# Two-layer decoder step on one core: gathered rows of layer 0 freed later, number pairs from their own tile, rows held back at the norms

## The chip, the cores and the metric

The kernel runs on one core of a Trainium2 chip as one program. The metric is the device time of one execution in microseconds. The kernel before took 3266.15, 3272.88 and 3274.58 us in three runs, a median of 3272.88. A profiled execution of it took 3263.07 us, of which the span from the first to the last recorded instruction is 3261.4 us.

The core has these engines, each with a queue of its own that is worked off strictly in order: PE (TensorE, matrix products), DVE (VectorE), ACT (ScalarE), POOL (GpSimd, here almost only for issuing gathers) and SP (SyncE, which issues the plain DMAs). An instruction waits at the head of its queue for semaphores that other engines raise; whatever stands behind it waits too.

## The reference

One step of a decoder with two layers, over 512 prompt tokens and 8 sample tokens, 1024 wide, in float32:

```
layer 0:  x += gmlp(rmsnorm(x));             x += peer(rmsnorm(x))
layer 1:  x += diff_attention(rmsnorm(x));   x += peer(rmsnorm(x))

rmsnorm:  y = x * rsqrt(mean(x*x) + EPS) * g

peer:     q  = h @ w_q                       # 8 heads, two halves of 128
          s  = q . keys                      # 128 + 128 scores for each head
          the 16 best of each half, the 16 best sums of pairs -> 16 of 16384 experts
          g  = softmax(the 16 sums)
          act = gelu(u_tab[expert] . h)
          out = sum over 8*16 experts of  g * act * v_tab[expert]
```

So each token picks 8 x 16 experts of 16384 in each layer; an expert is one row of `u_tab` and one of `v_tab`, 1024 numbers each. Outputs are the new x, the new keys and values, and a state of the gMLP.

## The kernel before

**Tiles.** The 512 prompt tokens are four tiles x0 to x3 of 128 tokens, the samples a fifth. Each layer's front (gMLP or attention, then the query and the ranking of `peer_front`) runs in two groups: in layer 0 first tile 2, then tiles 0, 1, 3 and the samples; in layer 1 first tile 0, then 2, 3, 1.

**Two ways to the experts.** In each layer two tiles (0 and 1 in layer 0, 2 and 3 in layer 1) go the *dense* way, `dense_peer`: all 16384 experts are computed on PE, and the 128 chosen ones get their weight by a one-hot product, the gates. The other two tiles go the *gathered* way, `peer_tile`: for each of the 128 choices POOL gathers a row of `u_tab` for each of the 128 tokens (0.5 MB for a tile), DVE multiplies and sums it (L712), and later the same for a row of `v_tab`, which DVE adds to x (L719). That is 2 x 256 = 512 such DVE instructions of 1024 columns for a layer; the text calls each of them a *gathered row*. They go through five buffers (`gb`).

**The dense way** runs in four quarters of 32 blocks of 128 experts. `acts(q)` computes the activations W: for q = 0 plain products (L494), after that with operands split in two (L209 on ACT and L211 on DVE make the high and low half, L488, L489 and L491 are the products). `gates(q)` builds one-hot tables: for 32 tokens at a time DVE compares the chosen row numbers with 0, 1, ..., 31, two tokens side by side (L512), scales that by the two parts of the gate (L514), and PE multiplies it with a second one-hot table (`ohj`, L520 on DVE or L526 and L529 on ACT) into L533; DVE multiplies the result into W (L536). Then PE multiplies W with the rows of `v_tab` (L573), in the last quarter with both sides split in two (L569 to L571; L564 makes the low half of W, L211 that of `v_tab`, each through two pairs of buffers). `gates(q+1)` and `acts(q+1)` run between the products of quarter q.

**The ranking** of a tile is DVE work: searches for the 8 largest and their places in score tiles `s_uv` and the like (L366 to L395, `topk_rank`), then the pick (L408 to L451, `topk_pick`), which goes to ACT for one Exp. For a dense tile PE transposes the pick (`ps_sel`, L461), for the samples L692.

**What sets the order.** The gathered rows have no fixed place in DVE's queue. While the body is written down, `tick` appends instructions to a list of anchors, each k times, and `peer_tile` collects the rows (`pins`). At the end `pace` ties row n to the n-th anchor: it may not be placed ahead of it. That sets the order in which a scheduler, with a clock of its own, places instructions; no semaphore comes of it. More ticks on an instruction free more rows there. In layer 0 the anchors begin when the ranking of tile 2 is through and go on into the first group of layer 1, until `cur[0] = None`; all rows of layer 0 must be done before group 2 of layer 1 reads x2 and x3.

**The norms** end in `rstd`, a chain of 8 or 9 small DVE instructions for the reciprocal root (L128 to L140).

Of the kernel before, what the change touches and what calls it, by code (L numbers as in the profile page):

```python
# [11 lines left out]
HF = mybir.dt.float16  # L12
# [3 lines left out]
OP = mybir.AluOpType  # L16
# [19 lines left out]
def body(ctx: ExitStack, tc: tile.TileContext, a):  # L36
    nc = tc.nc
    V, SC, PE, GP, SY = nc.vector, nc.scalar, nc.tensor, nc.gpsimd, nc.sync
# [37 lines left out]
    stage, dd = [0], {}  # L76
# [27 lines left out]
    def tick(ins, k=1):  # L104
        if cur[0] is not None:
            anchors[cur[0]].extend([ins.ins.name] * k)

    def pace():
        for a_, p_ in zip(anchors, pins):
            for n, ins in enumerate(p_):  # L110
                tc.add_manual_dep(ins, a_[min(n, len(a_) - 1)], NOSYNC, reason="pace")


    def small(p, m, name, dt=F32, bufs=4):
# [8 lines left out]
    def rstd(ss, p, m, inv_n, out=None):  # L123
        ms = small(p, m, "rs_ms" + ("m" if m > 1 else ""), F32, 1 if m > 1 else 4)
        y = small(p, m, "rs_y" + ("m" if m > 1 else ""), F32, 1 if m > 1 else 6)
        t = small(p, m, "rs_t" + ("m" if m > 1 else ""), F32, 1 if m > 1 else 4)
        u = small(p, m, "rs_u" + ("m" if m > 1 else ""), F32, 1 if m > 1 else 4)
        V.tensor_scalar(ms, ss, inv_n * KAP, EPS * KAP, op0=OP.mult, op1=OP.add)  # L128
        V.tensor_scalar(y.bitcast(I32), ms.bitcast(I32), -0.5, C0, op0=OP.mult, op1=OP.add)
        for k in range(2):  # L130
            if m == 1:
                V.scalar_tensor_tensor(t, y, y, ms, op0=OP.mult, op1=OP.mult)
            else:
                V.tensor_tensor(t, y, y, op=OP.mult)
                V.tensor_tensor(t, t, ms, op=OP.mult)
            if k == 0:
                V.scalar_tensor_tensor(y, t, -C2, y, op0=OP.add, op1=OP.mult)
        V.scalar_tensor_tensor(u, t, -CA, t, op0=OP.add, op1=OP.mult)
        out = y if out is None else out
        V.scalar_tensor_tensor(out, u, CB, y, op0=OP.add, op1=OP.mult)  # L140
        return out

    def bcast_row(src, n, name, bufs=2, p=128):
# [63 lines left out]
    def split(w, k=1):  # L207
        wh = wp.tile([128, 8, 128], FR, name="wh", tag="wh", bufs=2)
        SC.activation(wh, w, AF.Copy)  # L209
        wl = wp.tile([128, 8, 128], FR, name="wl", tag="wl", bufs=2)  # L210
        tick(V.tensor_tensor(wl, w, wh.bitcast(F32), op=OP.subtract), k)  # L211
        return wh, wl

    def dense(w, nk, rhs, n, consume, f0=0, f1=None, steps=None):

        f1 = w.shape[0] if f1 is None else f1
        for f in range(f0, f1):
            ps = pm.tile([128, 512], F32, name="ps_d", tag="mm")
            for c0 in range(0, nk, 8):
                wt = wp.tile([128, 8, 128], F32, name="wt", tag="wt")  # L220
                SY.dma_start(wt, w[f, :, c0:c0 + 8, :])
                if isinstance(rhs, list):
                    wh, wl = split(wt, [1, 2, 1, 2][stage[0]])
                    for c in range(8):
                        PE.matmul(ps[:, :n], wh[:, c, :], rhs[0][:, c, :n], start=c == 0, stop=False)
                        PE.matmul(ps[:, :n], wh[:, c, :], rhs[1][:, c, :n], start=False, stop=False)
                    for c in range(8):
                        PE.matmul(ps[:, :n], wl[:, c, :], rhs[0][:, c, :n], start=False, stop=c == 7)
                else:
                    for c in range(8):  # L230
                        z = PE.matmul(ps[:, :n], wt[:, c, :], rhs[:, c0 + c, :n], start=c0 + c == 0,  # L231
                                      stop=c0 + c == nk - 1)
                    tick(z, [6, 6, 6, 3][stage[0]])
            consume(f - f0, ps)
            step([4, 6, 4, 5][stage[0]] if steps is None else steps)

# [232 lines left out]
    def dense_peer(layer, dpa, open_rest, open_odd, smp):  # L469
        hT = dd["hT"]  # L470
# [7 lines left out]
        def acts(q):  # L478

            W[q] = (odd if q % 2 else dpa).tile([128, QI, 256], F32, name="W", tag="W", bufs=1)  # L480
            for il in range(QI):
                u = wp.tile([128, 8, 128], F32, name="ub", tag="wt")
                SY.dma_start(u, a["peer_ut"][layer, q * QI + il].rearrange("p (c e) -> p c e", c=8))
                ps = pt.tile([128, 512], F32, name="ps_a", tag="tr")[:, :256]
                if q:
                    uh, ul = split(u, [2, 3][layer])
                    for c in range(8):
                        PE.matmul(ps, uh[:, c, :], hP[0][:, c, :], start=c == 0, stop=False)  # L488
                        PE.matmul(ps, uh[:, c, :], hP[1][:, c, :], start=False, stop=False)  # L489
                    for c in range(8):  # L490
                        PE.matmul(ps, ul[:, c, :], hP[0][:, c, :], start=False, stop=c == 7)  # L491
                else:
                    for c in range(8):
                        z = PE.matmul(ps, u[:, c, :], hT[:, c, :256], start=c == 0, stop=c == 7)  # L494
                    tick(z, [0, 1][layer])
                    if il == 1:
                        SC.activation(hP[0], hT[:, :, :256], AF.Copy)
                        V.tensor_tensor(hP[1], hT[:, :, :256], hP[0].bitcast(F32), op=OP.subtract)
                SC.activation(W[q][:, il, :], ps, AF.Gelu_apprx_tanh)  # L499
                yield  # L500

        def gates(q):

            selJ, selb = dd["sel"]
            sq = dpb.tile([128, 256], HF, name="selq", tag="selq", bufs=1)
            V.tensor_scalar(sq, selb[:, 0, :], float(-q * QI), None, op0=OP.add)
            for t0 in range(0, 256, 32):

                gi = dpb.tile([128, 2, 16, QI, 2], HF, name="gi", tag="gi", bufs=2)
                sv = [z[:, t0:t0 + 32].rearrange("p (m w) -> p m w", w=2)[:, :, None, :].to_broadcast([128, 16, QI, 2])  # L510
                      for z in (sq, selb[:, 2], selb[:, 3])]
                V.tensor_tensor(gi[:, 1], sv[0], iotaJ[:, None, :QI, :2].to_broadcast([128, 16, QI, 2]), op=OP.is_equal)  # L512
                for k in range(2):
                    V.tensor_tensor(gi[:, k], gi[:, 1], sv[1 + k], op=OP.mult)  # L514
                for t1 in range(t0, t0 + 32, 16):
                    ps = pt.tile([128, QI, 16], F32, name="ps_g", tag="tr")
                    for t2 in range(t1, t1 + 16, 8):
                        oh = dpb.tile([128, 128, 8], HF, name="ohj", tag="ohj", bufs=4)
                        if (t2 // 8) % 4 < ([2, 2][layer] if not q else 2 * J_DVE[layer][q]):
                            V.tensor_tensor(oh, selb[:, 1, None, t2:t2 + 8].to_broadcast([128, 128, 8]), iotaJ,  # L520
                                            op=OP.is_equal)
                        else:

                            oh = oh.rearrange("p j k -> p (j k)").rearrange("p (k j) -> p j k", k=8)
                            for k in range(8):
                                SC.activation(oh[:, :, k], iota128, AF.Abs, scale=-1.0,  # L526
                                              bias=selJ[:, t2 + k:t2 + k + 1])
                            oh2 = oh.rearrange("p j k -> p k j")
                            SC.activation(oh2, oh2, AF.Relu, bias=1.0, scale=-1.0)  # L529
                        for k in range(8):  # L530
                            t = t2 + k
                            for c in range(2):
                                PE.matmul(ps[:, :, t - t1], oh[:, :, k], gi[:, c, (t - t0) // 2, :, t % 2], start=c == 0,  # L533
                                          stop=c == 1)
                    wv = W[q][:, :, t1:t1 + 16]
                    tick(V.tensor_tensor(wv, ps, wv, op=OP.mult), [3, 1][layer] if q else [5, 3][layer])  # L536
                    yield

        for _ in acts(0):
            step(4)  # L540
        drain()
        dpb, py = open_rest()
        y = [[py.tile([128, 512], F32, name=f"y{t}{hf}", tag=f"y{t}{hf}") for hf in range(2)] for t in range(2)]
        odd = open_odd()
        na = acts(1)
# [43 lines left out]
    def peer_front(tiles, n, layer, ph):  # L589
# [39 lines left out]
        for sp in range(4):  # L629
# [6 lines left out]
            def q_out(ft, ps):  # L636
                SC.activation(qT[:, o + ft, :n], ps[:, :n], AF.Copy)

            dense(a["peer_wq"][layer], 8, hT, n, q_out, sp * 4, sp * 4 + 4, [5, 2, 4, 3][stage[0]])
            for t in tiles:  # L640
                c0 = col(t)
                if t < 4:
# [560 lines left out]
```

## Time and profile before

| | before |
|---|---|
| median of three runs | 3272.88 us (3266.15 to 3274.58) |
| profiled execution, and its span | 3263.07 us, 3261.4 us |
| PE busy | 2977.0 us, 91% |
| DVE busy | 2450.0 us, 75% |
| ACT busy / POOL busy | 1379.5 us / 1369.9 us, 42% each |
| moved by DMA | 976.54 MB, 299 GB/s in the mean |
| gathered rows on DVE | 512 + 512, 615.5 and 655.7 us busy |

Times in rows are us from the start of the span. [...] A busy PE is not a PE at its peak, and an idle engine costs something only if another waits for it.

Where the stages lie: group 1 of layer 0 up to about 160, its group 2 with the gMLP to 434, the query and the ranking of four tiles from 434 to 741, with the last score search at 586; first gates 741 to 860, the dense stage to 1496, its last quarter to 1590. Layer 1: the projections of group 1 1590 to 1650, its attention and ranking to 1775, the projections of group 2 to 1915, its attention to 2100, ranking 2165 to 2320, then the dense way to the end.

### The profile page before, as it was taken

How to read it: one execution, taken by the hardware profiler on the slowest of the kernel's cores; microseconds unless marked ns; L12 is line 12 of the kernel's file. 1: busy time of each engine (PE TensorE's matmuls, PEld its weight loads, DVE VectorE, ACT ScalarE, POOL GpSimd, SP SyncE). 2: the span in 40 equal slices, each digit the busy share in tenths (PEclk: the TensorE clock that was granted, in tenths of full speed). 3: DMA queues.
4: the chain of work that ended last, by engine and by line, in shares of the span. 5: the costliest groups of instructions: out<-in, count | busy, mean ns of one | idle time of the engine just before them, and what ended most of it. 6: DMA issues, size and time to landing. Idle time of an engine off the chain costs nothing.

```text
span 3261.4 us, 50069 instructions
## 1 busy us (share of the span) xinstructions
PE 2977.0 (91%) x18048; PEld 2228.5 (68%) x18048; DVE 2450.0 (75%) x5093; ACT 1379.5 (42%) x3154; POOL 1369.9 (42%) x1061
## 2 busy tenths in 40 slices
PE   7998979758999999998998987688799999999999
PEld 7898646658747856856897643455688658768757
DVE  1489789989987678676425688869989887697775
ACT  2344021225677277386453233321236533353434
POOL 0045663455665446351000666544334564354340
PEclk9999989888999999999999988699899999999999
DMA  7788987888999989995655989877778999999885
GB/s 252 230 289 306 340 311 258 302 322 296 333 391 370 352 320 366 361 323 185 203 170 178 362 313 317 281 270 244 279 278 298 341 371 370 323 317 361 322 306 165
DMA packets 271563, 976.54 MB, mean 299 GB/s; under 512 B 30938, under 2 KB 31770, under 8 KB 271306
## 3 DMA queue, kind: packets, MB, share of 16 engines
q0 software_dynamic: 152064, 553.72, 46.9%
q1 hardware_dynamic: 119250, 419.62, 36.5%
q8 instruction: 142, 2.33, 0.3%
q14 instruction: 107, 0.88, 0.1%
HBM read 966.76 MB, written 6.46 MB: 298 GB/s over the span
## 4 chain that ended last, share of the span: by engine, by line
PE 53%; DVE 13%; DMA 11%; issue 11%; POOL 6%; ACT 5%; SPq 0%; POOLq 0%; DVEq 0%; ACTq 0%
PE y L573 13%; PE ps_d L231 7%; POOL gath L703 6%; DMA gath<-peer_u,ix 4%; PE ps_a L488 4%; PE ps_a L489 4%; PE ps_a L491 4%; DMA gath<-peer_v,ix 4%; PE ps_g L533 3%; PE ps_a L494 2%; DVE gath L712 2%; ACT ohj L526 2%; DVE x L719 2%; PE y L569 2%; PE y L570 2%
## 5 line engine op out<-in xcount | busy, mean ns | idle before, releaser
L703 POOL DMA_INDIRECT gath<-peer_u,ix x512 | 664.8, 1298 | 1077.6 <-DVE ix L671 490.5
L703 POOL DMA_INDIRECT gath<-peer_v,ix x512 | 666.5, 1302 | 669.9 <-DVE x L719 355.3
L719 DVE SCALAR_TENSOR_TENSOR x<-gath,act,x 128x1024 f32<-128x1024 f32 x512 | 655.7, 1281 | 72.4 <-DMA gath<-peer_v,ix 66.9
L573 PE MATMUL y<-vb,W 128*128 128x512 f32 x1536 | 699.5, 600 | 2.7 <-DMA vb<-peer_v 1.4
L712 DVE SCALAR_TENSOR_TENSOR gath<-gath,h_g 128x1024 f32<-128x1024 f32 x512 | 615.5, 1218 | 110.4 <-DMA gath<-peer_u,ix 108.9
L526 ACT ACTIVATE ohj<-iota,selJ 128x128 f16<-128x128 f32 x1408 | 425.7, 390 | 174.3 <-PE ps_g L533 174.1
L573 PEld LDWEIGHTS y<-vb,W 128*128 128x128 f32 x1536 | 280.7, 191 | 297.3 <-issue 290.4
L231 PE MATMUL ps_d<-hT,wt 128*128 128x128 f32 (+3 forms) x2048 | 429.1, 367 | 27.2 <-DMA wt<-peer_wq 6.9
L488 PE MATMUL ps_a<-hPh,wh 128*128 128x256 f32 x1536 | 403.2, 299 | 13.1 <-ACT wh L209 13.1
L231 PEld LDWEIGHTS ps_d<-hT,wt 128*128 128x128 f32 x2048 | 302.8, 197 | 139.3 <-issue 20.6
L489 PE MATMUL ps_a<-hPl,wh 128*128 128x256 f32 x1536 | 384.7, 287 | 0.0
L211 DVE TENSOR_TENSOR wl<-ub,wh 128x1024 fp32r<-128x1024 f32 x192 | 234.6, 1223 | 160.1 <-ACT wh L209 145.2
L209 ACT ACTIVATE wh<-ub 128x1024 fp32r<-128x1024 f32 x192 | 202.3, 1054 | 298.9 <-PE ps_a L489 274.1
L488 PEld LDWEIGHTS ps_a<-hPh,wh 128*128 128x128 f32 x1536 | 299.9, 195 | 27.7 <-ACT wh L209 15.5
L489 PEld LDWEIGHTS ps_a<-hPl,wh 128*128 128x128 f32 x1536 | 299.8, 195 | 10.1 <-issue 10.1
L494 PE MATMUL ps_a<-hT,ub 128*128 128x256 f32 x1024 | 232.6, 389 | 31.9 <-ACT W L499 31.9
L494 PEld LDWEIGHTS ps_a<-hT,ub 128*128 128x128 f32 x1024 | 199.1, 196 | 62.0 <-ACT W L499 32.7
L533 PEld LDWEIGHTS <-ohj 128*128 128x128 f16 x4096 | 180.7, 121 | 86.9 <-issue 46.5
L499 ACT ACTIVATE W<-ps_a 128x256 f32<-128x256 f32 x256 | 95.9, 379 | 329.2 <-PE ps_a L491 150.1
L491 PE MATMUL ps_a<-hPh,wl 128*128 128x256 f32 x1536 | 226.2, 290 | 3.6 <-DVE wl L211 3.6
L533 PE MATMUL ps_g<-gi,ohj 128*128 128x32 f16 x4096 | 190.4, 204 | 33.6 <-ACT ohj L529 19.0
L491 PEld LDWEIGHTS ps_a<-hPh,wl 128*128 128x128 f32 x1536 | 200.9, 193 | 13.5 <-issue 8.4
(298 smaller groups left out, 3840.4 us busy)
## 6 DMA issues: line engine op xcount, KB each, us to landing
ub<-peer_ut SPq DMA_DIRECT2D x256, 512.0 KB, 6.6
vb<-peer_v SPq DMA_DIRECT2D x256, 512.0 KB, 6.5
wt<-w_in SPq DMA_DIRECT2D x64, 512.0 KB, 4.7
wt<-peer_wq SPq DMA_DIRECT2D x64, 512.0 KB, 4.7
wt<-w_out SPq DMA_DIRECT2D x32, 512.0 KB, 5.0
gath<-peer_u,ix POOLq DMA_INDIRECT x512, 7.1
gath<-peer_v,ix POOLq DMA_INDIRECT x512, 7.2
wt<-w_k SPq DMA_DIRECT2D x16, 512.0 KB, 4.0
```

The lines of the kernel that those rows point to most:

```text
L211: tick(V.tensor_tensor(wl, w, wh.bitcast(F32), op=OP.subtract), k)
L231: z = PE.matmul(ps[:, :n], wt[:, c, :], rhs[:, c0 + c, :n], start=c0 + c == 0, stop=c0 + c == nk - 1)
L488: PE.matmul(ps, uh[:, c, :], hP[0][:, c, :], start=c == 0, stop=False)
L489: PE.matmul(ps, uh[:, c, :], hP[1][:, c, :], start=False, stop=False)
L491: PE.matmul(ps, ul[:, c, :], hP[0][:, c, :], start=False, stop=c == 7)
L494: z = PE.matmul(ps, u[:, c, :], hT[:, c, :256], start=c == 0, stop=c == 7)
L526: SC.activation(oh[:, :, k], iota128, AF.Abs, scale=-1.0, bias=selJ[:, t2 + k:t2 + k + 1])
L533: PE.matmul(ps[:, :, t - t1], oh[:, :, k], gi[:, c, (t - t0) // 2, :, t % 2], start=c == 0, stop=c == 1)
L573: PE.matmul(y[t][hf], w[:, ts], v[:, hs], start=i == 0, stop=i == 127)
L703: GP.indirect_dma_start(out=t, out_offset=None, in_=table, in_offset=bass.IndirectOffsetOnAxis(ap=ix[:, k:k + 1], axis=0))
L712: z = V.scalar_tensor_tensor(u, u, 1.0, h, op0=OP.mult, op1=OP.mult, accum_out=act[:, k:k + 1])
L719: z = V.scalar_tensor_tensor(x[t], v, act[:, k:k + 1], x[t], op0=OP.mult, op1=OP.add)
```

## The change

Three things are changed.

*Ticks.* The query products of `peer_front` free no rows in layer 0 any more (6 each before; 3 in layer 1, as before). In layer 0 the split operands of quarter 1 free 1 row instead of 2, the products into W free 4, 7, 3, 3 in quarters 0 to 3 instead of 5, 3, 3, 3.

*Holds.* `rstd` hands its last instruction to `hold`, which notes it with the place of the anchor list at that moment less 10. In `pace` the 20 rows from there on must not be placed ahead of that instruction: the ten that the anchors had last freed, and the ten next.

*Number pairs.* The comparison of the gate tables reads 0, 0, 1, 1, 2, 2, ... from a new tile `iotaP` (two copies of each number side by side) instead of the first two of eight copies in `iotaJ`. The tile is filled once a layer by a copy.

```diff
+    holds = [[], []]
+    def hold(ins, k=10):
+        if cur[0] is not None:
+            holds[cur[0]].append((len(anchors[cur[0]]) - k, ins.ins.name))
     def pace():
-        for a_, p_ in zip(anchors, pins):
+        for a_, p_, h_ in zip(anchors, pins, holds):
             for n, ins in enumerate(p_):
                 tc.add_manual_dep(ins, a_[min(n, len(a_) - 1)], NOSYNC, reason="pace")
+                for k, name in h_:
+                    if k <= n < k + 20:
+                        tc.add_manual_dep(ins, name, NOSYNC, reason="hold")
...
-        V.scalar_tensor_tensor(out, u, CB, y, op0=OP.add, op1=OP.mult)
+        hold(V.scalar_tensor_tensor(out, u, CB, y, op0=OP.add, op1=OP.mult))
...
-                    tick(z, [6, 6, 6, 3][stage[0]])
+                    tick(z, [6, 6, 6, 3][stage[0]] if ticks is None else ticks)
...
-                    uh, ul = split(u, [2, 3][layer])
+                    uh, ul = split(u, [[1, 2, 2], [3, 3, 3]][layer][q - 1])
...
-                V.tensor_tensor(gi[:, 1], sv[0], iotaJ[:, None, :QI, :2].to_broadcast([128, 16, QI, 2]), op=OP.is_equal)
+                V.tensor_tensor(gi[:, 1], sv[0], iotaP[:, None, :QI, :].to_broadcast([128, 16, QI, 2]), op=OP.is_equal)
...
-                    tick(V.tensor_tensor(wv, ps, wv, op=OP.mult), [3, 1][layer] if q else [5, 3][layer])
+                    tick(V.tensor_tensor(wv, ps, wv, op=OP.mult), [[4, 7, 3, 3], [3, 1, 1, 1]][layer][q])
...
+        iotaP = dpb.tile([128, 128, 2], HF, name="iotaP")
+        V.tensor_copy(iotaP, iotaJ[:, :, :2])
...
-            dense(a["peer_wq"][layer], 8, hT, n, q_out, sp * 4, sp * 4 + 4, [5, 2, 4, 3][stage[0]])
+            dense(a["peer_wq"][layer], 8, hT, n, q_out, sp * 4, sp * 4 + 4, [5, 2, 4, 3][stage[0]], 3 * layer)
```

Line numbers of the changed kernel are 10 higher up to the gate tables and 13 higher behind them: L712 and L719 are L725 and L732 there.

What moves in DVE's queue, at three places. First the pick of layer 0's last dense tile, before (`oh` is the table in which the pick looks up numbers, L446 and L447 sum it):

```order
L443 TENSOR_TENSOR oh<-oh,tmp 128x2048
L712 SCALAR_TENSOR_TENSOR gath,act<-gath,h_g 128x1024
L429 TENSOR_TENSOR tmp<-pos,tmp 128x8x16
L446 TENSOR_TENSOR oh<-oh 128x1024
L712 SCALAR_TENSOR_TENSOR gath,act<-gath,h_g 128x1024
L446 TENSOR_TENSOR oh<-oh 128x512
L446 TENSOR_TENSOR oh<-oh 128x256
L712 SCALAR_TENSOR_TENSOR gath,act<-gath,h_g 128x1024
L447 TENSOR_TENSOR tmp<-oh 128x16x8
```

And the same steps now:

```order
L453 TENSOR_TENSOR oh<-oh,tmp 128x2048
L439 TENSOR_TENSOR tmp<-pos,tmp 128x8x16
L456 TENSOR_TENSOR oh<-oh 128x1024
L456 TENSOR_TENSOR oh<-oh 128x512
L456 TENSOR_TENSOR oh<-oh 128x256
L457 TENSOR_TENSOR tmp<-oh 128x16x8
```

The gathered rows between the steps of the pick are gone from this place.

Second the last quarter of layer 0's dense way, before (`wdl` and `wl` are the low halves of W and of the rows of `v_tab`; the numbers tell one block from the next):

```order
L564 TENSOR_TENSOR wdl_12009<-W_9628,wdh_12007 128x256
L211 TENSOR_TENSOR wl_12005<-vb_12001,wh_12003 128x1024
L564 TENSOR_TENSOR wdl_12031<-W_9628,wdh_12029 128x256
L211 TENSOR_TENSOR wl_12027<-vb_12023,wh_12025 128x1024
L564 TENSOR_TENSOR wdl_12053<-W_9628,wdh_12051 128x256
```

Now:

```order
L577 TENSOR_TENSOR wdl_12011<-W_9630,wdh_12009 128x256
L221 TENSOR_TENSOR wl_12007<-vb_12003,wh_12005 128x1024
L725 SCALAR_TENSOR_TENSOR gath_13833,act_13232<-gath_13833,h_g_3106 128x1024
L725 SCALAR_TENSOR_TENSOR gath_13836,act_13232<-gath_13836,h_g_3106 128x1024
L577 TENSOR_TENSOR wdl_12033<-W_9630,wdh_12031 128x256
L221 TENSOR_TENSOR wl_12029<-vb_12025,wh_12027 128x1024
L725 SCALAR_TENSOR_TENSOR gath_13839,act_13232<-gath_13839,h_g_3106 128x1024
L577 TENSOR_TENSOR wdl_12055<-W_9630,wdh_12053 128x256
```

Before, no gathered row of layer 0 was left here; now one or two stand in each step.

Third the norm of the keys in group 2 of layer 1, before (`hss` is the sum of squares, `rs_` the chain of the root):

```order
L671 SCALAR_TENSOR_TENSOR ix<-tmp 128x128
L712 SCALAR_TENSOR_TENSOR gath,act<-gath,h_g 128x1024 x16
L716 TENSOR_TENSOR act<-act,gate 128x16
L719 SCALAR_TENSOR_TENSOR x_76<-gath,act,x_76 128x1024 x2
L346 TENSOR_REDUCE hss_16205<-junkh 128x16
L719 SCALAR_TENSOR_TENSOR x_76<-gath,act,x_76 128x1024
L346 TENSOR_REDUCE hss_16205<-junkh 128x16
```

Now:

```order
L684 SCALAR_TENSOR_TENSOR ix<-tmp 128x128
L725 SCALAR_TENSOR_TENSOR gath,act<-gath,h_g 128x1024 x2
L356 TENSOR_REDUCE hss_16207<-junkh 128x16 x3
L138 TENSOR_SCALAR rs_msm<-hss_16207 128x48
L139 TENSOR_SCALAR rs_ym<-rs_msm 128x48
L144 TENSOR_TENSOR rs_tm<-rs_ym 128x48
```

The rows that stood ahead of the sums and among the chain now stand behind the chain.

## Rows read from the trace of the kernel before

**Rows 1.** The page, busy time of each engine, share of the span, instructions.

```profile
PE 2977.0 (91%) x18048; PEld 2228.5 (68%) x18048; DVE 2450.0 (75%) x5093; ACT 1379.5 (42%) x3154; POOL 1369.9 (42%) x1061
```

**Rows 2.** Table by stage: stretch, length, engines' busy time, clock, DMA share, GB/s.

```profile
434.00:586.00 152.00, 127.24 (x480) 83.38 (x480) 138.70 (x584) 24.19 (x56) 61.65 (x53) 0.89 0.77 272
586.00:741.00 155.00, 105.43 (x458) 91.04 (x458) 139.78 (x372) 34.77 (x73) 85.12 (x66) 0.83 0.90 321
741.00:860.00 119.00, 110.41 (x1100) 105.94 (x1100) 114.64 (x150) 77.23 (x176) 67.53 (x46) 0.95 0.87 304
860.00:1496.00 636.00, 609.80 (x4172) 413.40 (x4172) 478.31 (x606) 416.86 (x1024) 326.13 (x255) 0.99 0.94 349
1496.00:1590.00 94.00, 93.64 (x400) 75.16 (x400) 52.83 (x67) 42.90 (x67) 0.00 (x0) 0.97 0.54 174
1590.00:1650.00 60.00, 55.69 (x461) 53.64 (x462) 19.33 (x46) 27.52 (x88) 0.00 (x0) 0.97 0.63 203
...
1775.00:1915.00 140.00, 138.59 (x489) 84.76 (x490) 105.72 (x183) 40.51 (x91) 78.24 (x60) 0.98 0.83 307
1915.00:2100.00 185.00, 134.38 (x405) 59.17 (x403) 159.65 (x382) 70.78 (x176) 106.27 (x86) 0.76 0.89 311
...
2165.00:2320.00 155.00, 125.03 (x463) 78.82 (x461) 138.97 (x624) 19.26 (x46) 62.68 (x52) 0.92 0.73 261
```

**Rows 3.** Waits of PE in 586:741: for whom, us in total, times, longest.

```profile
PE ps_sel L461 <- DVE tmp L447: 21.6, 2, 13.0
PE ps_ix L692 <- DVE tmp L687: 21.2, 1, 21.2
```

**Rows 4.** Timeline of ACT at 585: start, us; in brackets idle before, releaser.

```profile
585.81 0.38 ACT L499 ACTIVATE W<-ps_a 128x256 f32<-128x256 f32 x1 [23.00 <-DVE si L369]
```

**Rows 5.** DVE's costliest groups in 586:741: count, busy us, mean ns, idle before.

```profile
L719 DVE SCALAR_TENSOR_TENSOR x<-gath,act,x 128x1024 f32<-128x1024 f32 x33 | 42.1, 1275 | 0.0
L712 DVE SCALAR_TENSOR_TENSOR gath<-gath,h_g 128x1024 f32<-128x1024 f32 x30 | 36.4, 1216 | 10.0 <-DMA gath<-peer_u,ix 10.0
```

**Rows 6.** PE's costliest group in 586:733.

```profile
L494 PE MATMUL ps_a<-hT,ub 128*128 128x256 f32 x448 | 103.7, 396 | 13.3 <-ACT W L499 13.3
```

**Rows 7.** Timeline of DVE at 433, between L138 and L140.

```profile
433.00 1.22 DVE L712 SCALAR_TENSOR_TENSOR gath<-gath,h_g 128x1024 f32<-128x1024 f32 x1
```

**Rows 8.** Groups of the whole span: the gate tables on DVE.

```profile
L514 DVE TENSOR_TENSOR gi<-gi,selb 128x1024 f16<-128x1024 f16 x128 | 87.5, 686 | 0.6
...
L512 DVE TENSOR_TENSOR gi<-selq,iotaJ 128x1024 f16<-128x1024 f16 x64 | 69.2, 1083 | 0.0
```

**Rows 9.** DVE's costliest groups in 1496:1590.

```profile
L211 DVE TENSOR_TENSOR wl<-vb,wh 128x1024 fp32r<-128x1024 f32 x30 | 36.8, 1226 | 15.9 <-ACT wh L209 15.9
L564 DVE TENSOR_TENSOR wdl<-W,wdh 128x256 fp32r<-128x256 f32 x32 | 13.5, 426 | 23.3 <-ACT wdh L562 18.0 <-PE y L571 5.3
```

**Rows 10.** Timeline of ACT and DVE at 1502, in the last quarter.

```profile
1501.72 1.06 ACT L209 ACTIVATE wh<-vb 128x1024 fp32r<-128x1024 f32 x1 [1.19 <-PE y L571]
...
1502.82 1.23 DVE L211 TENSOR_TENSOR wl<-vb,wh 128x1024 fp32r<-128x1024 f32 x1 [0.60 <-ACT wh L209]
```

**Rows 11.** DMA queue of the weights in 1590:1650: packets, MB, share.

```profile
q1 hardware_dynamic: 3341, 12.11, 62.6%
```

**Rows 12.** Table by 50 us, columns as in rows 2: a stretch full of gathers.

```profile
350.00:400.00 50.00, 50.00 (x166) 29.35 (x165) 35.50 (x50) 2.17 (x6) 32.97 (x26) 1.00 1.00 377
```

**Rows 13.** Timeline of DVE: layer 1's first gathered row; the first sum for the keys.

```profile
1798.94 1.23 DVE L712 SCALAR_TENSOR_TENSOR gath<-gath,h_g 128x1024 f32<-128x1024 f32 x1 [7.24 <-DMA gath<-peer_u,ix]
...
1833.41 1.21 DVE L346 TENSOR_REDUCE hss<-junkh 128x16 f32<-128x1024 f32 x1
```

**Rows 14.** Waits of PE in 1915:2100.

```profile
PE ps_at L911 <- DVE p_sm L907: 13.4, 7, 3.9
PE ps_sc L895 <- DVE mx L871: 11.0, 5, 5.3
```

**Rows 15.** Waits of PE in 2165:2330.

```profile
PE ps_a L494 <- ACT W L499: 18.7, 1, 18.7
```

More of the change, by code (lines that the diff above doesn't have):

```diff
@@ L212, in split, with dense @@
         return wh, wl
-    def dense(w, nk, rhs, n, consume, f0=0, f1=None, steps=None):
+    def dense(w, nk, rhs, n, consume, f0=0, f1=None, steps=None, ticks=None):
         f1 = w.shape[0] if f1 is None else f1
```

## The prediction

> **What bounds the kernel now.** I read the page's busy times first: PE is busy 91% of the 3261.4 us span, DVE 75% [rows 1]. Such an average hides the stages, so the table by stage came next [rows 2]; in it one compares, for each stretch, its length with PE's busy time and DVE's. In 860:1496 (dense experts of layer 0) PE works 609.80 of 636 us and DVE 478.31: PE bounds, DVE has room. In 586:741 (the tail of the ranking) PE works 105.43 of 155 us and DVE 139.78: DVE bounds, PE stands still for 50 us. In 1496:1590 PE works 93.64 of 94 us and DVE only 52.83. Third, the waits of PE in 586:741: 21.6 us on the last step of a tile's pick (L447) and 21.2 us on the sample rows' (L687), both on DVE [rows 3]. ACT, too, whose eviction at 585.81 lets PE go on, had waited 23.00 us for a DVE index search, L369 [rows 4]. Fourth, what DVE does in the tail: 33 + 30 gathered rows, 42.1 + 36.4 us [rows 5]. Nothing there needs them; they stand in DVE's one queue between steps that are needed.
>
> So a gathered row costs DVE 1.28 us, and costs the kernel something only where an operation queued behind it is late. The question is where the rows go.
>
> **The change, part by part.** I counted in the two orders how many of layer 0's 512 rows stand in front of a given instruction of DVE. Last search of a score tile, L369: 160 before, 151 now. First gate table, L512: 222 before, 152 now. From there to the last gates of layer 0 the distance stays 76 to 79, whatever the new tick numbers: in the dense stage the pace is the same. First step of the last quarter (L564): 512 before, 435 now. End of layer 0: 512 and 479. First attention score of layer 1: 512 in both. So some 60 rows leave the ranking's tail, 44 enter the last quarter and 33 layer 1's first front.
>
> (1) *The tail of the ranking.* Without its 63 rows DVE has 139.78 - 78.5 = 61 us to do there. PE's own work is the 105.43 us, 103.7 of them the 448 products L494 [rows 6], which need none of the picks. So PE bounds, and 155 becomes 106: a gain of 49. Ends: 39, if DVE's 10 us of idle [rows 5] stay with PE, and 50. [...]
> (2) *The ranking before it.* In 434:586 DVE is busy nearly throughout, and a row or two leave it; in the norm ahead of it one row stood between the last two steps of the root and does no more [rows 7], as in the gMLP's norm at 255. I take 5 (0 to 10).
> (3) *The first gates, 741:860.* DVE is busy 114.64 of 119 us. It has 49 rows instead of 53 (5 us) and cheaper gate tables. L512 takes 1083 ns; L514, of the same size and types but without iotaJ, takes 686 [rows 8]. With the pairs side by side I take 690, so 0.4 us each, 3 us for the eight of this quarter and 25 us of DVE time in all 64, most of it where PE bounds and DVE's time is worth nothing. PE idles 8.6 us in the stage, so 0 to 8; I take 5. The copy into iotaP (256 elements, twice) lies beside L494 in PE's queue; without that cover it is less than one L514, 0.69 us.
>
> [...]
>
> (4) *The last quarter.* PE does 32 steps in its 93.64 us, without a gap, 2.9 us each. A step needs one L211 and one L564 of DVE, 1.226 + 0.426 us [rows 9]. A new row takes 1.28 and there are 1.4 for each step: 52.83 + 44 x 1.28 = 109 us in 94. DVE becomes the bound: 15 us lost at least. At most, one row delays L211 on every step: L211 starts at 1502.82, right behind ACT's copy, which ends at 1502.78 [rows 10], so nothing lies ready ahead of it; 32 x 1.28 = 41. Most rows stand behind L211, ahead of the next L564, so I stay near the floor: 18.
> (5) *Layer 1's first front, 1590:1650.* 33 rows add 42 us to DVE's 19.33: 61 in 60. Their bytes, 33 x 0.524 = 17.3 MB, come on top of 12.11 MB of weights [rows 11]. At the best pace shown with gathers, 377 GB/s and 26 rows in 50 us [rows 12], the 29.4 MB take 78 us and the rows 63. Five rows and four weight tiles can be loaded ahead. Ends 2 and 18; I take 8.
> (6) *Holding rows for the norms of layer 1.* In front of the key norm's sums DVE did 18 rows between 1798.94 and 1833.41 [rows 13]; now it does two and idles. Counted in the order, 19 rows fewer stand before that norm's root, 17 before the first score (572, now 555), 10 before the ranking's norm (676, now 666), none before its first scan (688 in both). Seven come back in the attention, 1915:2100, where DVE works 159.65 of 185 us and PE waits on it for 13.4 and 11.0 us [rows 14]: 9 us, less DVE's idle. Ten come back between that norm and the ranking, 2165:2320 [rows 2], where DVE bounds again (138.97 of 155) and whose end, through ACT, releases PE after 18.7 us [rows 15]: 10 x 1.28 to 10 x 50/26, so 13 to 19, less DVE's idle. At the projections, 1775:1915, PE works 138.59 of 140 us, so an earlier root saves little. I take 14 lost (0 to 28), less 2 for cheaper gate tables.
>
> Sum: -49 - 5 - 5 + 18 + 8 + 12 = -21 us. 860:1496 is PE's own and stays, and so I take layer 1's dense stage. The profiled execution took 3263.07 us, so 3242; the median of the runs shown, 3272.88, is 9.8 higher, and so is the forecast: 3252.
>
> **Rivals.**
> *The costs are hidden* (0.17). In 860:1496 243 rows pass beside a PE that is hardly idle; the new ones may find such pauses. Against: 109 us do not go into 94. If (4) to (6) cost a third of 38, it is -46, 3227; at nothing, -59, 3214. I put it at 3222.
> *PE stays late in the tail* (0.17). The waits on the picks shrink only by half, since a pick also goes through ACT, behind 28 evictions of W. For it: DVE idled 10 us in this stage. Against: 61 us of DVE have over 40 of room. Term (1) becomes 28: 0, so 3273.
> *The last quarter takes back what the tail gave* (0.11), the case on the other side. L211's input and output have two buffers each, so a step that waits holds the next. If a gather lands late, DVE's queue stops at the row, and L211 behind it. At two row times on each step the quarter costs 32 x 2.56 = 82 instead of 18: +43, 3316. It makes the kernel slower from 49 us on, 1.5 us a step; I put it at 3290.
> *The gate table stays at 1083 ns* (0.05): the tile saves nothing, 3 us less here and 2 in layer 1, -16, 3257. [...]
> *The forecast* (0.50): -21, 3252; its own range 3236 to 3266.
>
> **How the numbers follow.** The measurement tells 0.3%, 10 us, from no change, so faster ends at 3263 and slower begins at 3283. Faster: 0.50 x 0.86 + 0.17 + 0.05 x 0.7 + 0.17 x 0.2 = 0.67. Slower: 0.11 x 0.7 + 0.17 x 0.2 + 0.50 x 0.01 = 0.11. The rest, 0.22, is the same. Range: 3218, in the midst of the hidden case, to 3288, above the case of a late PE and at the near edge of the slower one; about one in five is left out.
>
> **What would show it.** PE's waits on L447 and L687 in layer 0 gone and the first L533 some 55 us earlier (1, 2). L512 at about 690 ns (3). The last quarter at 3.5 us a step, DVE hardly idle (4). The first score of layer 1 some 8 us later, counted from the end of layer 0 (5). DVE idle before the key norm, and a longer wait of L494 on ACT in layer 1 (6). The forecast is wrong if the tail keeps a wait above 20 us, or if the last quarter stays at 2.9 us or goes above 4.4.

## The result: slower by 0.65%, and the profile after

The changed kernel takes 3297.6 us (median of 8 runs, 3285.57 to 3315.47), the kernel before 3272.99 us in runs on the same chip. The ratio is 1.0065, 95% interval 1.0043 to 1.0087. The prediction was 3252 us, range 3218 to 3288: it had the wrong sign and missed the range.

The profiled execution took 3296.84 us, 33.8 us more than that of before. The medians lie 24.6 us apart and the ratio is worth 21: the profile of before is 9.8 us below its median, so some 10 us of what the stages below add up to is scatter. The page's busy times tell almost nothing of it, since the same work is done:

```profile
PE 3001.7 (91%) x18048; PEld 2239.4 (68%) x18048; DVE 2424.9 (74%) x5095; ACT 1385.9 (42%) x3158; POOL 1354.6 (41%) x1061
```

DVE works 25 us less than in [rows 1], as the cheaper gate tables should make it (43.5 us instead of 69.2). So the table by stage again, with boundaries at the same PE instructions as in [rows 2] (tail of the ranking, first gates, dense stage, last quarter, layer 1's first front, then its attention of group 2, the output product and the ranking). The columns are the stretch, its length, the busy us and the instructions of PE, PEld, DVE, ACT and POOL, then PE's granted clock (1.00 is its full speed), the mean busy share of the 16 DMA engines and GB/s:

```profile
586.80:691.10 104.30, 100.64 (x458) 87.90 (x458) 67.98 (x275) 31.73 (x66) 2.48 (x3) 0.97 0.51 164
691.10:808.70 117.60, 110.56 (x1105) 106.23 (x1106) 104.42 (x132) 79.08 (x177) 48.08 (x37) 0.94 0.79 273
808.70:1452.20 643.50, 609.87 (x4169) 412.20 (x4168) 470.18 (x617) 417.71 (x1029) 323.99 (x261) 0.98 0.93 347
1452.20:1560.10 107.90, 97.60 (x400) 74.59 (x400) 101.97 (x128) 44.47 (x69) 66.58 (x47) 0.97 0.98 364
1560.10:1644.00 83.90, 65.98 (x466) 61.16 (x466) 58.43 (x96) 30.45 (x92) 34.62 (x28) 0.86 0.90 339
...
1909.40:2108.40 199.00, 139.83 (x407) 63.08 (x405) 170.59 (x395) 72.73 (x179) 119.78 (x96) 0.72 0.88 310
2108.40:2178.10 69.70, 57.19 (x211) 36.75 (x212) 44.10 (x71) 19.41 (x40) 33.37 (x25) 0.89 0.71 253
2178.10:2344.70 166.60, 130.25 (x463) 81.27 (x461) 149.66 (x638) 19.33 (x44) 71.93 (x61) 0.89 0.77 273
```

The tail became 50.6 us shorter; 49 were forecast. The last quarter is 13.9 us longer, layer 1's first front 23.9, the attention of group 2 14.0, the output product 4.7, its ranking 11.5. DVE is at 102 of 108 us in the last quarter (52.83 of 94 before), and the DMA engines at 0.98 (0.54).

The waits say the same. In the tail the two waits of PE in [rows 3] are gone. One is left there, at the tail's start, that of [rows 4] for the score search (columns: for whom, us, times, longest):

```profile
PE ps_a L504 <- ACT W L509: 14.2, 1, 14.2
```

In the last quarter, where PE had one wait of 1.2 us, it now waits for the low halves of DVE behind rows:

```profile
PE y L583 <- DVE wl L221: 7.3, 8, 2.4
PE y L582 <- ACT wh L219: 2.5, 2, 1.2
```

In layer 1's first front PE waits for the normed keys and queries:

```profile
PE ps_t L209 <- DVE kq_tok L362: 5.8, 1, 5.8
PE ps_t L209 <- DVE kq_tok L360: 4.0, 1, 4.0
```

And DVE, whose queue holds them behind gathered rows, waits for gathers to land:

```profile
DVE gath L725 <- DMA gath<-peer_u,ix: 9.6, 5, 3.3
```

In group 2 of layer 1 the hold does what the order said: DVE does two rows and then idles 26.84 us until the key norm's sums, where before it did 18 rows [rows 13] (timeline: start, us, operation, idle before):

```profile
1798.13 1.22 DVE L725 SCALAR_TENSOR_TENSOR gath<-gath,h_g 128x1024 f32<-128x1024 f32 x1 [1.25 <-DMA gath<-peer_u,ix]
...
1826.21 1.22 DVE L356 TENSOR_REDUCE hss<-junkh 128x16 f32<-128x1024 f32 x1 [26.84 <-ACT junkh L355]
```

Counted in the trace, 93 rows now fall into the attention (84 before), 24 into the output product (24) and 60 into the ranking (52). PE's longest waits in these three, one of each:

```profile
PE ps_sc L908 <- DVE mx L884: 13.9, 7, 6.2
...
PE ps_t L209 <- DVE o_tok L360: 18.8, 1, 18.8
...
PE ps_ss L670 <- DVE qz L667: 12.9, 5, 4.4
```

Before, the first was 11.0 us [rows 14], the second, the output's norm, 11.7 and the third, an operand of the samples' scores, 2.8. So the first explains little: of the attention's 14.0 us, PE is busy 5.5 longer, at a granted clock of 0.72 instead of 0.76 [rows 2], and idle 8.6 longer, in many small waits. At the end of the ranking, PE's wait on ACT did not grow but shrank, from 18.7 us [rows 15]:

```profile
PE ps_a L504 <- ACT W L509: 13.7, 1, 13.7
```

The gate tables behave as reckoned:

```profile
L522 DVE TENSOR_TENSOR gi<-selq,iotaP 128x1024 f16<-128x1024 f16 x64 | 43.5, 682 | 0.0
```

682 ns instead of 1083 [rows 8], the price of L514. The comparison reads the same numbers, from pairs that begin 2 numbers apart instead of 8; by what means that spacing costs time was not shown.

### The profile page after: what moved, and what is told of

Its sections match the earlier page's. It is cut to its first block, busy times and chain, and to the rows that moved or that the text cites. A ratio compares the mean times of both kernels' runs of the same rounds, so it can differ in the third digit from the quotient of the medians.

```text
span 3295.1 us, 50077 instructions
## 1 busy us (share of the span) xinstructions
PE 3001.7 (91%) x18048; PEld 2239.4 (68%) x18048; DVE 2424.9 (74%) x5095; ACT 1385.9 (42%) x3158; POOL 1354.6 (41%) x1061
## 4 chain that ended last, share of the span: by engine, by line
PE 52%; DVE 13%; issue 13%; DMA 10%; POOL 6%; ACT 6%; another core or an unknown queue 0%; SPq 0%; POOLq 0%; DVEq 0%; ACTq 0%
PE y L586 13%; POOL gath L716 6%; PE ps_d L241 5%; PE ps_a L504 5%; PE ps_a L498 5%; PE ps_a L499 5%; PE ps_a L501 5%; DMA gath<-peer_u,ix 5%; PE ps_g L543 3%; DMA gath<-peer_v,ix 3%; ACT ohj L536 3%; DVE gath L725 2%; DVE x L732 2%; DVE si L379 1%; PE y L583 1%
## 5 line engine op out<-in xcount | busy, mean ns | idle before, releaser
L716 POOL DMA_INDIRECT gath<-peer_u,ix x512 | 656.1, 1282 | 966.9 <-DVE ix L684 335.3
L725 DVE SCALAR_TENSOR_TENSOR gath<-gath,h_g 128x1024 f32<-128x1024 f32 x512 | 616.1, 1220 | 120.3 <-DMA gath<-peer_u,ix 114.4
L732 DVE SCALAR_TENSOR_TENSOR x<-gath,act,x 128x1024 f32<-128x1024 f32 x512 | 655.5, 1280 | 55.8 <-DMA gath<-peer_v,ix 48.3
L241 PE MATMUL ps_d<-hT,wt 128*128 128x128 f32 (+3 forms) x2048 | 436.3, 372 | 27.3 <-DMA wt<-peer_wq 5.5
L498 PE MATMUL ps_a<-hPh,wh 128*128 128x256 f32 x1536 | 401.1, 298 | 10.4 <-ACT wh L219 10.4
L498 PEld LDWEIGHTS ps_a<-hPh,wh 128*128 128x128 f32 x1536 | 299.7, 195 | 23.2 <-ACT wh L219 12.6
L504 PE MATMUL ps_a<-hT,ub 128*128 128x256 f32 x1024 | 229.4, 386 | 28.5 <-ACT W L509 27.9
```

Of the source, the lines that this page charges most:

```text
L716: GP.indirect_dma_start(out=t, out_offset=None, in_=table, in_offset=bass.IndirectOffsetOnAxis(ap=ix[:, k:k + 1], axis=0))
L725: z = V.scalar_tensor_tensor(u, u, 1.0, h, op0=OP.mult, op1=OP.mult, accum_out=act[:, k:k + 1])
L732: z = V.scalar_tensor_tensor(x[t], v, act[:, k:k + 1], x[t], op0=OP.mult, op1=OP.add)
```

## The experiments

Each kernel was timed in five rounds against the kernel before on the same chip; chips differ (the kernel before has medians of 3265.8, 3279.3 and 3280.5 us in the three sets), so the ratio counts. The table gives, for the profiled execution of each, by how many us a stage is longer than in the profile of before, from the starts of the same PE instructions. Profiles of other chips differ too: runs 5 to 7 are the changed kernel itself up to the last quarter, yet are 10 to 13 us late at 586 (changed kernel 1) and lose 10 to 13 in the dense stage (7.5). A profile is also one execution of several: that of run 5 lies 13 us above its median, that of run 4 10 us below, so a column need not add up to its ratio. Only larger differences, or those found in one place again and again, are read from it.

| stage (before's us) | changed | 1 no holds | 2 holds | 3 pairs | 4 three ticks | 5 no gather | 6 thin | 7 head holds | 8 spread | 9 two ticks |
|---|---|---|---|---|---|---|---|---|---|---|
| to 586 | 0.8 | -7.8 | 4.0 | -0.2 | 0.1 | 12.1 | 12.9 | 10.4 | 3.4 | -1.1 |
| tail, 586:741 | -50.6 | -50.4 | -2.9 | -3.7 | -21.5 | -51.2 | -51.2 | -51.0 | -36.8 | -39.0 |
| first gates, :860 | -1.4 | -0.2 | 2.5 | -0.3 | -5.6 | -2.6 | -2.6 | -2.7 | -2.0 | -1.8 |
| dense 0, :1496 | 7.5 | 5.4 | 5.2 | 1.2 | -8.8 | 10.2 | 13.1 | 11.4 | 13.0 | 10.0 |
| last quarter, :1590 | 13.9 | 19.7 | 0.2 | 0.4 | 8.8 | 23.4 | 13.3 | 12.6 | -0.1 | 12.1 |
| front 1, :1650 | 23.9 | 15.1 | 0.1 | -0.5 | -0.3 | -0.1 | 17.2 | 22.7 | 19.1 | 0.4 |
| :1915 | 0.4 | 2.1 | -0.8 | -1.8 | 0.3 | 2.0 | -1.2 | -0.7 | 12.4 | 4.0 |
| attention, :2100 | 14.0 | 1.4 | 8.5 | -0.6 | 0.2 | 18.2 | 18.0 | 7.2 | 7.0 | -1.7 |
| output, :2165 | 4.7 | -0.5 | 0.8 | -0.1 | -0.1 | 4.0 | 1.6 | 4.8 | -0.4 | -0.4 |
| ranking, :2320 | 11.5 | 1.2 | 12.1 | -0.6 | -0.2 | 14.5 | 13.8 | -1.2 | 3.0 | 3.8 |
| to the end | 9.1 | -2.0 | 6.0 | -2.5 | -3.6 | 11.4 | 8.8 | 3.5 | 9.8 | 11.2 |
| ratio to before | 1.0065 | 0.9967 | 1.0102 | 0.9989 | 0.9936 | 1.0035 | 1.0080 | 1.0030 | 1.0014 | 0.9923 |

**1. The changed kernel without the holds.**

```diff
-        hold(V.scalar_tensor_tensor(out, u, CB, y, op0=OP.add, op1=OP.mult))
+        V.scalar_tensor_tensor(out, u, CB, y, op0=OP.add, op1=OP.mult)
```

> The changed kernel without the holds; ticks and number pairs stay. Changed kernel: 3297.6 us. Theory A (the holds push 17 gathered rows of layer 1 out of the norms of group 2 into its attention and ranking, where DVE is full): the 30 us that these two stages lost (1910 to 2345 in the changed kernel) come back, and some 5 us more since 26 rows are left for layer 1's first front instead of 33: about 3262. Theory B (the 30 us come of the late start of layer 1's rows and of fuller DMA queues, not of the holds): 3290 to 3298.

Ratio 0.9967 (0.9950 to 0.9984): faster than before. Against 3273 us that is 3262, the number of theory A. Attention, output and ranking of layer 1 are back at before's length. So ticks and pairs alone gain 0.3%, and the holds turn that into a loss. In layer 0 the holds only move rows: the last quarter loses 19.7 us here (13.9 with them) and layer 1's first front 15.1 (23.9), together about the same.

**2. The kernel before with the holds alone** (ticks and tables as before).

> The kernel before with the holds alone (both layers). Before: 3273 us. Theory A: the attention and ranking of layer 1 become 25 to 30 us longer, little happens in layer 0 (its rows end in front of the last quarter but for 4): 3298 to 3303. Theory B: 3273, since its rows come no later to layer 1.

Ratio 1.0102 (1.0074 to 1.0130), some 33 us: theory A again, a little above its range. 8.5 us fall into the attention, 0.8 into the output product and 12.1 into the ranking: 21, where theory A has 25 to 30. Some 14 us more stand in other stages, 6 of them behind the ranking and 9 in layer 0 up to its last quarter, which theory A doesn't explain. The scatter of the profiles is as large, and no run has the holds of layer 0 alone.

**3. The kernel before with the number pairs alone.**

> The kernel before with the number pairs from their own tile alone. The comparison takes 682 ns instead of 1083 (the changed kernel's trace), 0.4 us in each of 64, 26 us of DVE. If DVE's time counts only in the first gates of a layer (8 comparisons each): 3 us in each layer, 3267. If PE hides it wherever it stands: 3273. If shorter DVE work in the dense stages lets gathers start sooner there and takes bandwidth from the weights: above 3273.

Ratio 0.9989 (0.9971 to 1.0007): nothing that can be told from no change, and no loss of the third kind. 26 us of DVE time less are worth under 10 us.

**4. Three ticks for a query product, no holds.**

```diff
-            dense(..., [5, 2, 4, 3][stage[0]], 3 * layer)
+            dense(..., [5, 2, 4, 3][stage[0]], [3, 3][layer])
```

> The changed kernel without the holds and with 3 ticks for each query product of layer 0 instead of 0 (before: 6). In the order 40 of layer 0's rows stand between the last score search and the first gates (63 before, 1 in the changed kernel), 30 in the last quarter (0 before, 43 now), none in layer 1's first front (33 now). Theory C (what counts in each stage is the sum of DVE's work against PE's): the tail has 61 + 40 x 1.28 = 112 us of DVE beside 106 of PE, so it keeps some 42 of the 52 us won; the last quarter has 53 + 38 = 91 in 94, so it loses 0 to 5; the front loses none; 3273 - 42 - 3 + 4 = 3232. Theory D (each row that stands between two needed steps costs its own length, whatever room the stage has): the tail gives back 51 us, the last quarter costs 10: 3280.

Ratio 0.9936 (0.9913 to 0.9959), and 0.9929 (0.9903 to 0.9954) when it was run once more beside run 9. In time (0.9936 of 3273 is 3252) it lies between the two theories, and so does the tail, which kept 21.5 us, not 42. Its row in the table by stage has DVE at 115 of 133 us:

```profile
586.10:719.50 133.40, 105.75 (x458) 91.19 (x458) 115.32 (x345) 34.66 (x72) 58.52 (x45) 0.90 0.83 294
```

And PE waits for the last step of a pick again:

```profile
PE ps_sel L471 <- DVE tmp L457: 19.7, 2, 13.0
```

So 42 rows, counted in the trace, cost 29 us there, 0.7 us each. By the sums 35 of them would have been free (61 + 35 x 1.28 is PE's 106); theory C leaves out that in the order all of them stand ahead of the last picks, on which PE waits. The last quarter lost 8.8 us with 30 rows, above theory C's 0 to 5, though DVE has room there:

```profile
1460.10:1562.90 102.80, 95.59 (x400) 73.89 (x400) 86.45 (x114) 44.41 (x69) 35.72 (x27) 0.98 0.84 307
```

The front lost nothing.

**5 and 6. What a late row of layer 0 costs: DVE's time or the gather.** Run 5 leaves out the gathers of the last 77 rows and keeps DVE's time, run 6 does the reverse.

```diff
-                u = gather(a["peer_u"], ix, k)
...
+                late = not layer and len(pins[0]) >= 435
+                u = gb.tile([128, D], F32, name="gath", tag="g") if late else gather(a["peer_u"], ix, k)
...
-                v = gather(a["peer_v"], ix, k)
...
+                v = h if late else gather(a["peer_v"], ix, k)
```

> The changed kernel, in which the last 77 gathered rows of layer 0 (those from the last quarter on) gather nothing: DVE works through the same 1024 columns, on the normed tile that lies there anyway (their part of the result is left out). In the order 51 of them stand in the last quarter (43 in the changed kernel) and 16 in layer 1's first front (34). The changed kernel lost 14 us in that quarter and 24 in that front. Theory F (DVE's time makes the loss): the quarter has 53 + 65 = 118 us of DVE in 94, loses 20 or more; the front loses about half, 12: 3290. Theory G (the bytes and the landing of the gathers make it: the DMA engines are 0.98 and 0.89 busy there): nearly all 38 us come back, 3260. Both: between.

```diff
...
-                z = V.scalar_tensor_tensor(x[t], v, act[:, k:k + 1], x[t], op0=OP.mult, op1=OP.add)
+                c = 64 if not layer and len(pins[0]) >= 435 else D
+                z = V.scalar_tensor_tensor(x[t][:, :c], v[:, :c], act[:, k:k + 1], x[t][:, :c], op0=OP.mult, op1=OP.add)
```

> The changed kernel, in which the same 77 rows gather in full, but DVE works on 64 of the 1024 columns (the rest of their part of the result is left out); the places in the order are the changed kernel's. Theory F (DVE's time): the quarter and the front come back but for a few us, 3262. Theory G (bytes and landing of gathers): all of the loss stays, 3297.

The two stages give two answers. First run 5, last quarter and front:

```profile
1464.50:1581.90 117.40, 98.93 (x400) 77.55 (x400) 116.19 (x150) 45.07 (x70) 0.00 (x0) 0.91 0.44 139
1581.90:1641.80 59.90, 55.55 (x461) 53.52 (x462) 36.96 (x63) 28.04 (x88) 0.00 (x0) 0.97 0.63 204
```

And run 6:

```profile
1468.20:1575.60 107.40, 97.33 (x400) 73.93 (x400) 61.76 (x131) 44.47 (x69) 53.06 (x48) 0.98 0.99 376
1575.60:1652.80 77.20, 59.98 (x466) 56.07 (x466) 25.94 (x93) 29.96 (x92) 26.13 (x27) 0.96 0.92 354
```

*Last quarter.* Without gathers (57 rows by the trace, DMA share 0.44) DVE is busy 116 of 117 us and the loss is 23 us: DVE's time suffices to make it. With thin rows (46) DVE is busy 62 of 107 us, yet the loss stays 13 us: DMA share 0.99, 376 GB/s, so the gathers suffice too, by their bytes or by rows that have not landed (DVE waits for such rows 15 us there). The two runs are not quite at one load: the 11 rows that run 5 has more than run 6 are 14 us of DVE, without which its loss would be some 9 (an estimate). So either alone makes most of the 14 us, and taking away one brings little. *Front.* Without gathers, 14 rows of DVE time cost nothing at all. With thin rows 17 of 24 us stay, while DVE works only 26 of 77 us. It stands at rows that have not landed, as its waits in that front show:

```profile
DVE x L734 <- DMA gath<-peer_v,ix: 16.9, 9, 3.6
DVE gath L726 <- DMA gath<-peer_u,ix: 12.6, 6, 3.6
```

Behind these rows stand the norms of the keys and queries, for which PE waits: 9.8 us in the changed kernel (shown above), though only 4.6 of the 13 us that PE idles more in run 6; the rest there is spread over waits on ACT and on weights. So theory G holds in the front as to the gathers, and the path from them to PE is shown in part; of the 24 us some 7 go with DVE's time. Run 5 has 14 rows there instead of 32, so it shows only that DVE time at that load is free.

**7. Holds of layer 1 at the heads' norms only.**

```diff
-        hold(V.scalar_tensor_tensor(out, u, CB, y, op0=OP.add, op1=OP.mult))
+        z = V.scalar_tensor_tensor(out, u, CB, y, op0=OP.add, op1=OP.mult)
+        if cur[0] == 0 or m > 4:
+            hold(z)
```

> The changed kernel, with the holds of layer 1 at the norms of the heads (keys, queries, output of the attention) only, not at the norm ahead of the ranking. In the order the rows ahead of the latter's root are 676 again, as before (666 in the changed kernel), those ahead of the queries' root stay 538 (560 before), and of the output's 642 (652). The changed kernel lost 14 us in the attention, 5 behind it and 12 in the ranking. Theory H (each norm's ten rows cost where they come back): the ranking's 12 us come back, the attention's 19 stay: 3286. Theory I (the rows that the keys' and queries' norms set back are the ones that burden the ranking): all stays, 3297.

Ratio 1.0030 (1.0012 to 1.0047). The ranking is back, with 52 rows instead of 60, so the 8 rows that come back there had cost 12.7 us, 1.6 each:

```profile
2179.80:2333.60 153.80, 124.82 (x463) 78.70 (x461) 139.12 (x625) 19.38 (x46) 67.99 (x52) 0.91 0.73 263
```

Theory H, not I. The 8 rows stand in the output product now (32 instead of 24), which loses 4.8 us against 4.7; with 24 rows the other kernels with these holds (runs 2, 5 and 6) lose 0.8 to 4.0, so the 8 cost between nothing and 4 us. So the same rows, held, cost 1.6 us each or at most 0.5, by where they come back.

**8. Layer 0's late rows spread into the attention of layer 1** (no holds, two ticks, fewer in the dense stage).

```diff
-                    uh, ul = split(u, [[1, 2, 2], [3, 3, 3]][layer][q - 1])
+                    uh, ul = split(u, [[1, 1, 1], [3, 3, 3]][layer][q - 1])
...
-                    tick(V.tensor_tensor(wv, ps, wv, op=OP.mult), [[4, 7, 3, 3], [3, 1, 1, 1]][layer][q])
+                    tick(V.tensor_tensor(wv, ps, wv, op=OP.mult), [[4, 3, 2, 2], [3, 1, 1, 1]][layer][q])
```

> The changed kernel without the holds, with 2 ticks for a query product of layer 0, and fewer ticks in its dense stage. In the order 24 of layer 0's rows stand in the ranking's tail (1 in the changed kernel, 63 before), none in the last quarter (43), 21 in layer 1's first front up to the queries' root (24), and 35 in its attention and later, up to the ranking (0). It asks for the price of a row in that attention, where DVE is 47 of 125 us busy and the DMA engines 0.60. Against the kernel before: tail -33, dense stage -5, front +12. Theory J (a stage with room takes rows at no cost): attention 0 to 5, 3273 - 24 = 3249. Theory K (its chain from scores to products goes through DVE at every step, so that a row costs its length there): +45, 3292.

Ratio 1.0014 (0.9995 to 1.0032): the same as before. By the trace 30 rows fell into the front and 26 behind it. The front lost 19 us, the attention and ranking of group 1 13.2 us, 0.5 us a row: neither J nor K, and no cheaper than the last quarter (0.3 us a row in runs 4 and 9).

**9 and 10. Two ticks beside three, no holds.**

> As the run with half the ticks, but 2 for each query product of layer 0 instead of 3. In the order 24 rows stand in the ranking's tail (40 there), 42 in the last quarter (30), 3 in layer 1's first front (0). By the prices of a row that the runs so far show (tail: 29 us for 40 rows and 14 for 23, 0.6 to 0.7 us; last quarter: 9 for 30, 14 for 43, 20 for 46; front 0.6 to 0.9): tail 15 us better, quarter 5 to 6 worse, front 2 worse: 7 us below the run with 3 ticks, 0.991 to 0.992 of the kernel before. If the dense stage gives back what the tail gains (with no row in the tail it lost 5 us, with 40 it won 9): the same as with 3 ticks, 0.9936.

> The kernel with 3 ticks once more, beside the one with 2 on the same chip: 0.9936 of the kernel before, 0.991 to 0.996.

Ratio 0.9923 (0.9895 to 0.9952) for two ticks, 0.9929 for three: no difference. The tail is 16 us shorter with two (39.0 against 23.0 us won, in one set), and the dense stage of layer 0 gives it back (10.0 us lost against 4.7 won). PE's waits there for ACT's one-hot tables (L539) are 18.7 us against 11.6, half of the difference; but the kernel before has 19.0 (L529) and is 10 us faster there than two ticks, so they do not explain it. What does is open.

Either one, with ticks and pairs but no holds and a part of the rows left in the ranking, is the version that beats both kernels, by 0.6 to 0.8% the one before.

## Why the prediction was wrong

By its own sum, -21 us, against the 33.8 us of the profile (21 by the ratio):

- *(1) Tail, -49*: right, -50.6, with the cause named: PE's waits on L447 and L687 gone. PE's work took 100.6 us at a clock of 0.97 instead of 105.4 at 0.83, and PE still idled 3.7; the two, which the term left out, about cancel. Runs 4, 8 and 9 add that its sum, DVE's work against PE's, holds only for a nearly empty stage: by it 24 rows would cost nothing (61 + 31 us in 106), and they take 11 to 14 us back.
- *(2), (3) Ranking before, first gates, -10*: +0.8 (for all up to 586; about -2 from 434 on) and -1.4. L512's duration was right (690, measured 682), its worth was not: run 3 shows no gain that can be told.
- *(4) Last quarter, +18*: +13.9. Right in size, in part by luck. DVE is nearly full, as forecast, but the loss does not begin where its sum passes PE's: 30 rows make 91 us in 94 and lost 8.8 (run 4). And the gathers make most of the loss by themselves (run 6), which the term left out. The sum that term (5) uses would have shown them: 174 GB/s over 94 us [rows 2] are 16.4 MB, 44 rows 23.1 more, and at 377 GB/s the two take 105 us (an estimate).
- *(5) Layer 1's first front, +8*: +23.9, above its upper end of 18. **This step failed** in its choice: the term set the 61 us of DVE in 60 beside the bytes (78 us) and went near DVE's end. Runs 5 and 6 show the reverse: DVE's time is nearly free (14 rows of it cost nothing), and the stage pays for the gathers (17 of the 24 us stay without DVE's time). It took 83.9 us for 28.5 MB, at up to 422 GB/s in its fullest slices, 339 in the mean, with a share of 49.6% for gathers (q0) against 40.5% for the plain DMAs, weights above all (q1):

```profile
q0 software_dynamic: 4289, 15.60, 49.6%
q1 hardware_dynamic: 3639, 12.76, 40.5%
```

  The bytes alone, at the 377 GB/s of [rows 12], are 75 us; for the rest, a row that hasn't landed stops DVE's queue ahead of a norm, as the waits shown above say (9.6 us in five waits on rows of `peer_u`). Nor did the term have PE's clock, granted at 0.86 there instead of 0.97: the products, nearly the same in number, keep PE busy 66 us instead of 55.7 [rows 2], 10 of the 24 us. It fell where PE had just stood idle (busy 4.4 of the 10 us from 1590 to 1600 of the profile, then a clock of 0.71 to 1610). The gathers were not served behind the weights: in ten of its fullest us, 1590 to 1600 of the profile, q0 moved 2.17 MB and q1 2.02.
- *(6) Holds, +12*: +30.2 (14.0 + 4.7 + 11.5), just above its upper end of 28. **This step failed** in size: where the rows go was right (17 come back, by the trace 9 in the attention and 8 in the ranking), their price was not. Set off against DVE's idle time I took 14 us for 17 rows, 0.8 each; in the ranking it is 1.6 us (run 7), more than the row's own 1.28, and in the attention 0.7 to 1.6 (runs 7 and 2, changed kernel). Nor was the ranking's path right: the term had PE released later through ACT at its end, and that wait shrank from 18.7 to 13.7 us, while the wait for the samples' operand (L667) grew from 2.8 to 12.9. Run 2 shows the holds alone to cost 1.0%.
- *860:1496 and layer 1's dense stage, 0*: +7.5 and +9.1. Over the runs the two vary from -9 to +13 and from -4 to +11, on chips with kernels that hardly differ there. What sets it is open.

Of the rivals, none is what happened: the costs were not hidden, the tail was not late, the gate table did not stay at 1083 ns, and the last quarter did not take the gain back. The chance of a slower kernel hung nearly all on that quarter and on a late tail; no case had the loss in the front or at the norms. Nor did either of its signs of being wrong come: the tail's longest wait is 14.2 us and the quarter takes 3.4 us a step, both as forecast. Of the 55 us between the sum and the profile, 34 sit in terms (5) and (6), which I had at one third and two fifths of their size; 17 sit in the two dense stages, unexplained, and 9 in (2) and (3). With (5) and (6) at their measured size the sum is +13, against the ratio's 21. Without the holds, the forecast's own terms give -35, and run 1 measures -11 (0.9967): by its profile the front (15.1 for 8), the first gates (-0.2 for -5) and layer 0's dense stage (5.4 for 0) make most of that.

## What to carry to other kernels

Background work that is moved out of a late stage arrives in another one; ask there not only whether the engine has time, but whether its data will have landed: in run 6's first front DVE's queue stood still for 29.5 us at rows that had not, and whatever was behind waited too. Two loads that each nearly fill a stage (here DVE and the gathers in the last quarter) hid each other: taking away one showed little (a loss of 23.4 us without the gathers and of 13.3 without most of DVE's work, 13.9 with both). And a stage paid for such work before an engine was full: 30 rows cost 9 us where DVE had 86 of 103 (run 4). A hold that idles a cheap place gives the work back in a dear one, so price it where it comes back: the same eight rows cost 1.6 us each in a full ranking and at most 0.5 in a product stage with room.

## What was not expected of the hardware

Layer 1's first front kept 17 of its 24 us of loss when DVE's work on the late rows was cut to a sixteenth of the columns and DVE sat idle for two thirds of the time (run 6). And 26 us less work on an engine that is 75% busy changed the time by nothing that can be measured (run 3, ratio 0.9989).
